# One encoder layer: the general program moved between the main program and the closing blocks, with branch hints

## The chip, the cores and the metric

The kernel runs on one core of one Trainium2 chip. The core has five engines with instruction streams of their own: TensorE (PE; its weight loads are listed as PEld), VectorE (DVE), ScalarE (ACT), GpSimd (POOL) and SyncE (SP), which here issues nearly all DMAs. Each stream is read by a sequencer, which also runs branches, register loads and semaphore waits itself; the profile marks such work with a q (SPq, PEldq). [...] The metric is the device time of one execution in microseconds (us), and a shorter time is better.

## The reference

The layer works on 1024 positions of width 1024 in float32. Two mixers run on one projection: dense grouped-query attention with axial rotary positions, and a mixture of three dilated windows with a distance penalty. A feed-forward network with a short convolution follows.

```python
def reference(x, norm1_g, w_in, ..., conv_w, conv_b, w_down):
    hn = rms_norm(x, norm1_g)
    proj = hn @ w_in
    ...
    out_a = global_gqa_attention(qa, ka, va)
    out_b = dilated_mixture_attention(rms_norm(qb, qb_norm_g), rms_norm(kb, kb_norm_g), vb)
    mixed = jnp.concatenate([rms_norm(out_a, outa_norm_g), rms_norm(out_b, outb_norm_g)], axis=-1)
    x = x + mixed @ w_out
    x = x + conv_ffn(rms_norm(x, norm2_g), w_up, conv_w, conv_b, w_down)
    return x
```

The queries and keys of both mixers are normalised per head and multiplied by gain vectors. So the gains alone bound how large a score before the softmax can become.

## The kernel before

The kernel holds the whole layer twice. The function `emit(bounded)` (L142) writes one complete program for all engines. With `bounded=True` it writes the main program, which leaves out the subtraction of the row maximum before the exponentials, since the scores are known to be small. With `bounded=False` it writes the general program, which subtracts it and then computes the whole output again.

Which one counts is decided on the chip. `bound()` (L597) computes from the gains, near the start, an upper bound of the scores and stores it in one element of the SBUF tile `bigf` at `O_LIM`. The main program always runs. After it, each of the five engines loads that element into a register (`values_load`, L1610) and compares it with a limit (`tc.If`, L1612). If the bound is above the limit, the engine goes on into the general program; with the inputs used here it is not, and the general program is skipped.

The built program of each engine consists of blocks that lie one behind the other in memory. Five blocks matter:
- a short opening block (L1668, L1672);
- the main program, which ends with the register load and the branch of the If. On SP it has 745 instructions;
- the closing block of the main arm (L1612). It waits until this engine's work, and on SP every DMA of the main program, is done, sets the semaphores to the values that the general program would have left, and jumps to the end. On SP it has 9 instructions: eight waits and the jump;
- the general program (L1612 stands for its branch too). On SP it has 729 instructions, on PE 7040 before weight loads are counted apart;
- the end (L1672). SP waits there for all semaphores with twelve waits and a drain, then all engines pass two barriers, between which POOL clears the semaphores. On SP it has 17 instructions.

Before the change they lie in this order: opening, main program, closing block, general program, end. The argument `preferred_fallthrough_block=False` asks for it: the arm taken when the condition is false follows the branch directly. So the branch of the If falls through into the closing block, and the closing block's jump to the end passes over the whole general program.

The work around the end of the main program is a product of the feed-forward network's second weight with the gated activations, by a scheme with seven products in place of eight block products (`steps`, `down`, L1474). Its last step adds four parts of the output and writes them: `out_add` (L1469) adds on DVE (L1470) and starts the write from SP (L1472). The order of instructions within a block comes from a scheduler that keeps each engine's dependencies; a call of no dependency is placed where the scheduler sees fit, not where it was written.

The profile calls both conditional branches and plain jumps COMPARE_BRANCH, waits on semaphores EVENT_SEMAPHORE, and the register load TENSOR_LOAD. The transfers that bring instructions to the engines are the queues of kind "instruction": q8 for PE and q14 for the other engines.

Of the kernel before, what the change touches and what calls it, by code (L numbers as in the profile page):

```python
# [41 lines left out]
O_LIM = O_F + 9232  # L42
LIMIT = 256.0
# [83 lines left out]
def tile_encoder_layer(ctx, tc, x, w_in, gains, outg, norm1_g, norm2_g, w_out, w_up, conv_w, conv_b,  # L127
                       w_down, ident, rope, tmx, tbc, cnt, tee, out):
    nc = tc.nc
# [3 lines left out]
    bigf = pool.tile([128, NF], F32, name="bigf")  # L133
# [8 lines left out]
    def emit(bounded):  # L142
# [930 lines left out]
        def take(prep, n):  # L1073
            for _ in range(n):
                if prep:
                    p = prep.pop(0)
                    if p:
                        p()
# [296 lines left out]
        def conv(j, u):  # L1375
            c = tile_of(j, u)
            i = F_U[2 * (j % 2) + u]
            a = acc(j, u)
            w = [f(O_CW + 44 * t + c, 1) for t in range(4)]
            act(f(a, 1024), f(i, 1024), AF.Identity, scale=w[1], bias=w[3])  # L1380
            for w_, o, d, n in ((w[0], 256, 0, 768), (w[0], 1, 768, 255), (w[2], 0, 256, 768), (w[2], 768, 1, 255)):
                vec.scalar_tensor_tensor(f(a + o, n), f(i + d, n), w_, f(a + o, n), op0=OP.mult, op1=OP.add)  # L1382

        def gate(j, u):
            a, v = acc(j - 1, u), acc(j, u)
            act(f(a, 1024), f(a, 1024), AF.Gelu_apprx_tanh)
            vec.tensor_tensor(f(v, 1024), f(a, 1024), f(v, 1024), op=OP.mult)
# [5 lines left out]
        def gate_sums(j):  # L1393
            e, o = acc(j, 0), acc(j, 1)
            s1, s3 = acc(j - 1, 0), acc(j - 1, 1)
            t = lambda d, a, b, op: gp.tensor_tensor(f(d, 512), f(a, 512), f(b, 512), op=op)
            g = gscr[j // 2]

            def behind_sum(o):

                gp.tensor_tensor(f(o, 1), f(F_S[1], 1), f(F_S[1], 1), op=OP.add)

            def halves():
                dma(g[:, 0:512], f(e, 512))
                dma(g[:, 512:1536], f(o, 1024))
                behind_sum(s1)
                t(s1, e + 512, o + 512, OP.add)

            def third():
                behind_sum(s3)  # L1410
                t(s3, e, e + 512, OP.subtract)

            def second():
                t(s1 + 512, s1, e, OP.subtract)
                dma(g[:, 1536:2560], f(s1, 1024))

            def fourth():
                t(s3 + 512, o, s1 + 512, OP.subtract)
                dma(g[:, 2560:3584], f(s3, 1024))

            return [halves, second, third, fourth]
# [5 lines left out]
        steps = [(n, q) for n in (1, 5, 6, 3, 7, 2, 4) for q in range(NQ)]  # L1427
# [4 lines left out]
        def d_load(m):  # L1432
            if m >= len(steps):
                return
            n, q = steps[m]
            o = F_DR[m % 4]
            dma(f(o, 512), w_part(q, *{1: (0, 0), 5: (0, 1), 6: (1, 1), 3: (1, 1), 7: (1, 1), 2: (1, 0), 4: (1, 0)}[n]))
            dma(f(o + 512, 512), gscr[q][:, place[n]:place[n] + 512])

        def d_load2(m):  # L1440
            n, q = steps[min(m, len(steps) - 1)]
            if n in (5, 7):
                dma(f(F_D2[q % 3], 512), w_part(q, 0, n == 7))

        def d_prep(m):
            if m >= len(steps):
                return
            n, q = steps[m]
            o, d, t = F_DR[m % 4], R_D[m % 6], F_T[q]
            sub = lambda out, i0, i1: vec.tensor_tensor(f(out, 512), f(i0, 512), f(i1, 512), op=OP.subtract)  # L1450
            if n == 5:
                sub(t, o, F_D2[q % 3])
            elif n == 6:
                sub(t, o, t)
            elif n == 7:
                sub(o, o, F_D2[q % 3])
            elif n == 4:
                sub(o, o, t)
            src = fp(t, [o + 512 - t, 2], [1, 512]) if n in (5, 6) else fp(o, [512, 2], [1, 512])
            act(rp(d, [512, 2], [1, 512]), src, AF.Copy)  # L1460
            vec.tensor_tensor(rp(d + 1024, [512, 2], [1, 512]), src, rfp(d, [512, 2], [1, 512]), op=OP.subtract)  # L1461
# [4 lines left out]
        def x_rows(c, t, tt, hf):  # L1466
            dma(f(c[t], 512), rscr[tt][:, 512 * hf:512 * hf + 512])

        def out_add(c, t, b, tt=None, hf=0):  # L1469
            vec.tensor_tensor(f(c[t], 512), bank(b), f(c[t], 512), op=OP.add)  # L1470
            if tt is not None:
                dma(o_rows(tt, hf), f(c[t], 512))  # L1472

        def down(m):  # L1474
            n, q = steps[m]
            d = R_D[m % 6]
            for t in range(4):
                o = bank(t + 4 * (n in (5, 3, 2)))
                ah, al = r(d + 512 + 128 * t, 128), r(d + 1536 + 128 * t, 128)
                mm(o, ah, r(d, 512), start=(q == 0 and n in (1, 5, 2)), stop=False, skip_group_check=True)  # L1480
                mm(o, ah, r(d + 1024, 512), start=False, stop=False, skip_group_check=True)  # L1481
                mm(o, al, r(d, 512), start=False, stop=(q == NQ - 1), skip_group_check=True)  # L1482
                if n == 4 and q == NQ - 1:
                    out_add(C_12, t, t, 4 + t, 0)

        def behind(n, q):

            if q < 4:
                if n == 5:
                    out_add(C_11, q, q)  # L1490
                elif n == 6:
                    out_add(C_22, q, 4 + q)
                elif n == 3:
                    out_add(C_12, q, q)
                elif n == 7:
                    out_add(C_12, q, 4 + q, q, 1)
                elif n == 2:
                    out_add(C_22, q, q, 4 + q, 1)
                elif n == 4:
                    out_add(C_11, q, 4 + q, q, 0)  # L1500
            elif 4 < q < 9:
                t = q - 5
                if n == 1:
                    x_rows(C_11, t, t, 0)
                elif n == 5:
                    x_rows(C_22, t, 4 + t, 1)
                elif n == 6:
                    x_rows(C_12, t, t, 1)
                elif n == 2:
                    x_rows(C_12, t, 4 + t, 0)  # L1510
# [83 lines left out]
        for m in range(len(steps)):  # L1594
            n, q = steps[m]
            down(m)
            d_prep(m + 3)
            if m < 2:
                conv(last, m)
            if m == 2:  # L1600
                gate(last, 0)
                gate(last, 1)
            if m == 3:
                take(gate_sums(last), 4)
            d_load2(m + 6)
            d_load(m + 7)
            behind(n, q)

    emit(True)
    limit = nc.values_load(bigf[0:1, O_LIM:O_LIM + 1].bitcast(mybir.dt.int32), min_val=0, max_val=2 ** 31 - 1,  # L1610
                           skip_runtime_bounds_check_because="any float32 that is not negative is right")
    with tc.If(limit > int(np.float32(LIMIT).view(np.int32)), preferred_fallthrough_block=False):  # L1612
        emit(False)


# [60 lines left out]
```

## Time and profile before

| what | value |
|---|---|
| median of three runs | 1301.46 us (1300.12 to 1302.01) |
| profiled execution, device time | 1300.51 us |
| its span, first to last instruction of the program | 1298.7 us |
| PE busy | 1236.4 us, 95% of the span |
| DVE, ACT, POOL busy | 70%, 49%, 30% |
| granted TensorE clock, mean | 0.988 |
| instruction transfers on q8 | 57, 0.93 MB |
| instruction transfers on q14 | 45, 0.37 MB |

The span covers the program's own instructions; the execution's time has 1.8 us more around it. An engine is counted as busy only for work in its datapath: branches, waits, register loads and the issue of DMAs are not busy time, so a stretch in which only sequencers run shows as idle. Rows by source line give, for each engine and operation, the count, the shortest, median and longest duration in ns, and the starts of the first and the last one in us from the start of the span.

### The profile page before, as it was taken

How to read it: one execution, taken by the hardware profiler on the slowest of the kernel's cores; microseconds unless marked ns; L12 is line 12 of the kernel's file. 1: busy time of each engine (PE TensorE's matmuls, PEld its weight loads, DVE VectorE, ACT ScalarE, POOL GpSimd, SP SyncE). 2: the span in 40 equal slices, each digit the busy share in tenths (PEclk: the TensorE clock that was granted, in tenths of full speed). 3: DMA queues.
4: the chain of work that ended last, by engine and by line, in shares of the span. 5: the costliest groups of instructions: out<-in, count | busy, mean ns of one | idle time of the engine just before them, and what ended most of it. 6: DMA issues, size and time to landing. Idle time of an engine off the chain costs nothing.

```text
span 1298.7 us, 18774 instructions
## 1 busy us (share of the span) xinstructions
PE 1236.4 (95%) x7063; PEld 1061.5 (82%) x7063; DVE 908.5 (70%) x1270; ACT 637.4 (49%) x1001; POOL 391.8 (30%) x300
## 2 busy tenths in 40 slices
PE   7999999999998889999999999999999998889996
PEld 7999998999997777888788888888888886657885
DVE  5988685124107779656999999999999964657672
ACT  7856554566556566535544453444443442234430
POOL 1610143000212230011465675665675530000000
PEclk9999999999999899999999999999999998999998
DMA  7126303000014444413222223232223357448970
GB/s 264 54 84 156 88 5 75 24 17 17 9 25 100 106 107 115 156 65 106 74 105 91 92 93 122 94 117 90 91 96 122 122 183 282 166 148 277 315 242 36
DMA packets 120935, 147.12 MB, mean 113 GB/s; under 512 B 51009, under 2 KB 79489, under 8 KB 120321
## 3 DMA queue, kind: packets, MB, share of 16 engines
q1 hardware_dynamic: 119617, 141.10, 33.6%
q0 software_dynamic: 1216, 4.72, 1.7%
q8 instruction: 57, 0.93, 0.3%
q14 instruction: 45, 0.37, 0.1%
HBM read 107.25 MB, written 33.82 MB: 109 GB/s over the span
## 4 chain that ended last, share of the span: by engine, by line
PE 55%; DVE 18%; issue 4%; DMA 4%; ACT 3%; POOL 1%; SPq 0%; ACTq 0%; DVEq 0%; POOLq 0%
PE ps L696 8%; PE ps L1349 6%; PE ps L1351 6%; PE ps L1350 6%; DVE bigf L1382 6%; PE ps L1481 4%; PE ps L1482 4%; PE ps L1480 4%; PE ps L701 3%; PE ps L702 2%; DVE bigf L1353 2%; PE ps L1004 2%; PE ps L1006 2%; PE ps L1005 2%; DVE bigr L1333 2%
## 5 line engine op out<-in xcount | busy, mean ns | idle before, releaser
L1349 PE MATMUL ps<-bigr 128*128 128x512 f32 x616 | 241.0, 391 | 6.5 <-DVE bigf L1353 5.9
L1350 PE MATMUL ps<-bigr 128*128 128x512 f32 x616 | 239.7, 389 | 0.0
L1351 PE MATMUL ps<-bigr 128*128 128x512 f32 x616 | 239.7, 389 | 0.0
L1382 DVE SCALAR_TENSOR_TENSOR bigf<-bigf 128x768 f32<-128x768 f32 (+1 forms) x176 | 178.8, 1074 | 26.5 <-ACT bigf L1380 26.4
L1332 ACT ACTIVATE bigr<-bigf 128x512 fp32r<-128x512 f32 x154 | 93.2, 625 | 139.3 <-POOL bigf L1324 70.4
L1460 ACT ACTIVATE bigr<-bigf 128x1024 fp32r<-128x1024 f32 x77 | 80.5, 1058 | 148.9 <-DMA bigf<-gscr 57.1
L1349 PEld LDWEIGHTS ps<-bigr 128*128 128x128 f32 x616 | 115.6, 188 | 35.1 <-DVE bigf L1353 9.3
L696 PEld LDWEIGHTS ps<-bigf 128*128 128x128 f32 x1024 | 131.9, 191 | 9.3 <-issue 0.3
L1351 PEld LDWEIGHTS ps<-bigr 128*128 128x128 f32 x616 | 115.6, 188 | 24.2
L1350 PEld LDWEIGHTS ps<-bigr 128*128 128x128 f32 x616 | 115.7, 188 | 23.5
L1461 DVE TENSOR_TENSOR bigr<-bigf,bigr 128x1024 fp32r<-128x1024 f32 x77 | 93.2, 1222 | 57.0 <-ACT bigr L1460 46.8
L1480 PE MATMUL ps<-bigr 128*128 128x512 f32 x308 | 114.1, 401 | 16.6 <-ACT bigr L1460 16.4
L696 PE MATMUL ps<-bigf 128*128 128x65 f32 x1024 | 129.1, 269 | 0.0
L421 PE MATMUL ps<-bigr 128*128 128x256 f32 x448 | 127.3, 284 | 1.2 <-ACT bigf L300 1.2
L1333 DVE TENSOR_TENSOR bigr<-bigf,bigr 128x512 fp32r<-128x512 f32 x112 | 125.3, 1136 | 3.2 <-ACT bigr L1332 2.5
L422 PE MATMUL ps<-bigr 128*128 128x256 f32 x448 | 126.9, 283 | 0.1
L423 PE MATMUL ps<-bigr 128*128 128x256 f32 x448 | 126.7, 283 | 0.0
L1481 PE MATMUL ps<-bigr 128*128 128x512 f32 x308 | 122.6, 400 | 1.4 <-DVE bigr L1461 0.9
L1482 PE MATMUL ps<-bigr 128*128 128x512 f32 x308 | 121.3, 395 | 0.0
L704 ACT ACTIVATE bigf<-ps 128x512 f32<-128x512 f32 x128 | 76.1, 597 | 78.9 <-PE ps L702 77.9
L421 PEld LDWEIGHTS ps<-bigr 128*128 128x128 f32 x448 | 85.8, 192 | 1.8 <-ACT bigf L300 1.6
L422 PEld LDWEIGHTS ps<-bigr 128*128 128x128 f32 x448 | 85.9, 192 | 0.3 <-DVE bigr L405 0.3
(215 smaller groups left out, 2441.8 us busy)
## 6 DMA issues: line engine op xcount, KB each, us to landing
bigf<-w_down SPq DMA_DIRECT2D x99, 256.0 KB, 3.7
bigf<-w_up SPq DMA_DIRECT2D x44, 512.0 KB, 3.6
bigf<-gscr SPq DMA_DIRECT2D x77, 256.0 KB, 3.7
gscr<-bigf SPq DMA_DIRECT2D x33, 512.0 KB, 2.6
bigf<-w_in SPq DMA_DIRECT2D x8, 1024.0 KB, 5.5
bigf<-x SPq DMA_DIRECT2D x15, 512.0 KB, 7.1
bigf<-w_out SPq DMA_DIRECT2D x8, 512.0 KB, 3.6
bigr<-bigr POOLq DMA_DIRECT2D x8, 512.0 KB, 4.7
```

The costliest lines, as they stand in the source:

```text
L421: mm(o, ah, wh, start=(k == 0 and t % 2 == 0 and n != 2), stop=False, skip_group_check=True)
L422: mm(o, ah, wl, start=False, stop=False, skip_group_check=True)
L423: mm(o, al, wh, start=False, stop=(k == 3), skip_group_check=True)
L696: mm(bank(ob, 65, 66 * i), f(slots[kt] + 128 * i, 128), f(F_VA + 132 * kt + 66 * kv, 65), start=(kt == 0 and i == 0), stop=(kt == 7), skip ...
L1333: (gp if n in (2, 4) and m > 3 else vec).tensor_tensor(rp(o + 512, [128, 4], [1, 128]), src, rfp(o, [128, 4], [1, 128]), op=OP.subtract)
L1349: mm(bank(b), wh, th, start=(k == 0 and n in (1, 5, 6, 7)), stop=False, skip_group_check=True)
L1350: mm(bank(b), wh, tl, start=False, stop=False, skip_group_check=True)
L1351: mm(bank(b), wl, th, start=False, stop=(k == 3), skip_group_check=True)
L1382: vec.scalar_tensor_tensor(f(a + o, n), f(i + d, n), w_, f(a + o, n), op0=OP.mult, op1=OP.add)
L1480: mm(o, ah, r(d, 512), start=(q == 0 and n in (1, 5, 2)), stop=False, skip_group_check=True)
L1481: mm(o, ah, r(d + 1024, 512), start=False, stop=False, skip_group_check=True)
L1482: mm(o, al, r(d, 512), start=False, stop=(q == NQ - 1), skip_group_check=True)
```

## The change

The If gets the opposite preference and a label, the register load is called inside the last loop of the main program, in the last step but one, and at the same place a branch hint is marked for all five engines. It names the label and says "likely taken".

```diff
             d_load2(m + 6)
             d_load(m + 7)
             behind(n, q)
-
+            if bounded and m == len(steps) - 2:
+                limit.append(nc.values_load(bigf[0:1, O_LIM:O_LIM + 1].bitcast(mybir.dt.int32), min_val=0,
+                                            max_val=2 ** 31 - 1, skip_runtime_bounds_check_because="any float32 that is not negative is right"))
+                tc.mark_branch_hint_location("general", "LikelyTaken", mybir.ALL_ENGINES)
+
+    limit = []
     emit(True)
-    limit = nc.values_load(bigf[0:1, O_LIM:O_LIM + 1].bitcast(mybir.dt.int32), min_val=0, max_val=2 ** 31 - 1,
-                           skip_runtime_bounds_check_because="any float32 that is not negative is right")
-    with tc.If(limit > int(np.float32(LIMIT).view(np.int32)), preferred_fallthrough_block=False):
+    limit, = limit
+    with tc.If(limit > int(np.float32(LIMIT).view(np.int32)), preferred_fallthrough_block=True, label="general"):
         emit(False)
```

In the built program the blocks then lie in the order opening, main program, general program, closing block, end. The branch of the If falls through into the general program and is taken to the closing block, which the end follows directly. Each engine's stream has one more instruction, the prefetch hint, which stands first in the main program's block and names that engine's branch of the If. All other instructions, their order within their blocks and the semaphores they wait for are the same, the register load among them: it stands behind the last matmul, addition and output write of its engine, as before.

## The prediction

> **What bounds the kernel now.** I read the page first, for the busy shares and the instruction queues, then the table by stage, then the end of the chain of waits, and then, line by line, what the sequencers do after the last arithmetic.
>
> ```profile
> span 1298.7 us, 18774 instructions
> ...
> PE 1236.4 (95%) x7063; PEld 1061.5 (82%) x7063; DVE 908.5 (70%) x1270; ACT 637.4 (49%) x1001; POOL 391.8 (30%) x300
> ...
> q8 instruction: 57, 0.93, 0.3%
> q14 instruction: 45, 0.37, 0.1%
> ```
>
> ```profile
> 1065.00:1287.70 222.70, 203.91 (x849) 160.11 (x847) 126.26 (x139) 70.24 (x67) 1.94 (x2) 0.97 0.65 218
> 1287.70:1298.70 11.00, 0.00 (x0) 0.00 (x0) 0.00 (x0) 0.00 (x0) 0.00 (x0) 0.70 0.17 60
> ```
>
> TensorE (PE) bounds the kernel as a whole, but the change does not touch what PE computes. In the table by stage the columns are busy time and count of PE, PEld, DVE, ACT and POOL. Its last row matters here: for the final 11.0 us no engine is busy at all. The chain of waits does not show these 11 us, because it follows engine work only. It ends with the four last additions of DVE:
>
> ```profile
> 1284.65 0.24 PE ps L1482
> 1284.89 0.02 issue
> 1284.92 2.73 DVE bigf L1470 x4
> ```
>
> So 1284.92 + 2.73 = 1287.65 is the end of arithmetic, and 1298.7 the end of the program. What lies between is SyncE (SP): the last write of the output, the branch of the If, the waits that close the main arm, and the waits that close the program. First the last output write:
>
> ```profile
> L1472 SPq DMA_DIRECT2D out_dram<-bigf x1: 333/333/333, 1287.7 to 1287.7; - x1
> ...
> DMA to landing us min/median/max: 4.5/4.5/4.5
> ```
>
> It lands at 1287.7 + 4.5 = 1292.2. The rows of the If (L1612, count, duration in ns, first and last start) and those of the program's end (L1672, in two adjoining windows, then the final barrier):
>
> ```profile
> L1612 SPq EVENT_SEMAPHORE  x8: 17/17/17, 1291.5 to 1292.6; - x8
> L1612 PEldq COMPARE_BRANCH  x2: 95/2182/4270, 1283.3 to 1287.1; - x2
> L1612 DVEq COMPARE_BRANCH  x2: 51/53/55, 1287.9 to 1288.1; - x2
> L1612 SPq COMPARE_BRANCH  x2: 38/46/53, 1288.6 to 1292.7; - x2
> ...
> L1612 DVEq EVENT_SEMAPHORE  x1: 21/21/21, 1288.0 to 1288.0; - x1
> ```
>
> ```profile
> L1672 SPq EVENT_SEMAPHORE  x3: 28/28/28, 1295.2 to 1295.4; - x3
> ```
>
> ```profile
> L1672 SPq EVENT_SEMAPHORE  x9: 27/28/28, 1297.2 to 1297.8; - x9
> L1672 SPq DRAIN  x1: 7/7/7, 1297.8 to 1297.8; - x1
> ```
>
> ```profile
> L1672 PEldq EVENT_SEMAPHORE  x2: 51/51/51, 1298.1 to 1298.7; - x2
> ```
>
> The SP sequence is: first branch at 1288.6 (the If, not taken); eight waits that let go as the output lands, 1291.5 to 1292.6; second branch at 1292.7 (past the general program to the end); nothing until 1295.2; three waits; nothing from 1295.4 to 1297.2; nine waits at 0.07 us each ((1297.8 − 1297.2) / 8); drain at 1297.8; barriers to 1298.7. The two silences are 2.5 and 1.8 us, in which SP waits for no semaphore that is still open: the last writes landed at 1292.2 and the other engines arrived earlier (below). They coincide with transfers on the instruction queue. The next table has DMA share and GB/s as its last two columns; 82 GB/s over 0.1 us is 8,192 bytes, which is what q14 moves at a time (0.37 MB / 45):
>
> ```profile
> 1292.80:1293.60 0.80, 0.50 0.00 0
> 1293.60:1293.70 0.10, 0.50 0.24 82
> 1293.70:1295.20 1.50, 0.50 0.00 0
> 1295.20:1295.70 0.50, 0.50 0.00 0
> 1295.70:1295.80 0.10, 0.50 0.25 82
> 1295.80:1297.30 1.50, 0.50 0.00 0
> ```
>
> So both silences are SP waiting for code. A jump to the end block fetches its 8 KB line (2.5 us), and since the block straddles two lines, its fourth wait stands in the next one. That one is asked for only about 0.5 us after the first is entered (1295.2 to 1295.7) and is usable 2.0 us after it (1295.2 to 1297.2).
>
> **The change, part by part.** The built program shows what moves. Instructions of the main program and both arms are the same on every engine and in the same order; SP has 745 in the main program, 9 in the closing block of the main arm, 729 in the general program and 17 at the end, before and after.
>
> *The register load.* It is called earlier, but keeps its place: on SP behind the last output write, on PE behind the last matmul, on DVE behind the last addition. Cost and gain nothing. Even a move would gain nothing, since on SP it lies under the landing at 1292.2.
>
> *The hints.* One prefetch hint per engine is added. They were marked in the last step but one, but in the built program each is its engine's first instruction. SP's first DMA issue and all that hangs on it shift by one such instruction. None is in the trace, so I bound it: below by 0.02 us (SP's waits, 17 ns), above by 0.10 us (PE's first branch, 95 ns). A gain from an extra instruction at the head of an idle queue is excluded. I take 0.05 us, near the SP rows, as SP starts the first transfers.
>
> *The order of the blocks.* Before: main program, closing block of the main arm, general program, end. After: main, general, closing block, end. On the path taken, the far jump goes from "closing block to end" to "If to closing block", and the end then follows the closing block directly. On SP this far jump now starts at 1288.6 and must be over when the third output write lands at 1291.5; before, it started at 1292.7 with nothing left to cover it.
>
> If the hint brings the target line in ahead, SP is in the closing block at once, and the next line, asked for 0.5 us after entry and usable 2.0 us after it, is there at about 1290.7, ahead of its use. Then:
> - first silence: 2.5 becomes one step of 0.07 to 0.1 us: −2.4
> - second silence: 1.8 becomes one step of 0.07: −1.7
> - hints: +0.05
>
> Sum: −4.05. Counted forward instead, from 1292.7 on: twelve waits of 0.07 (0.8), 0.9 us from drain to end and the hint's 0.05 put the end at 1294.5, which is −4.2. I take −4.1.
>
> The far jump of the other engines moves too, so I check that none becomes last. Their arrivals at the end block now:
>
> ```profile
> L1672 DVEq DRAIN  x1: 57/57/57, 1291.3 to 1291.3; - x1
> L1672 PEldq DRAIN  x1: 68/68/68, 1291.4 to 1291.4; - x1
> ```
>
> ```profile
> L1612 POOLq COMPARE_BRANCH  x2: 38/39/40, 1065.0 to 1067.8; - x2
> ...
> L1672 POOLq DRAIN  x1: 1128/1128/1128, 1071.7 to 1071.7; - x1
> ```
>
> ```profile
> L1672 ACTq DRAIN  x1: 80/80/80, 1274.6 to 1274.6; - x1
> ```
>
> PE pays its far jump in the record of the branch itself, 4270 ns from 1287.1; moved to its If at 1283.3 it would end at 1287.6, under matmuls already queued. DVE's takes 3.2 us (1288.1 to 1291.3) and would now start at 1287.9. POOL's 3.9 us (1067.8 to 1071.7) has over 200 us of cover. If DVE also needed its next line, 1287.9 + 3.2 + 2.0 = 1293.1, still before SP's drain at 1293.6. ACT is there by 1274.6. So SP stays last, and the whole gain counts.
>
> *Without the hint's help* the If's jump misses on SP. The price is 2.5 us by SP's own row at a quiet time, and 3.2 by DVE's, which ran like this one while the output was being written. I take 3.2 for this case, as the nearest in time: SP resumes at 1288.6 + 3.2 = 1291.8, 0.3 after the first landing but before the second. The next line is there at 1291.8 + 2.0 = 1293.8. The end block grows no longer, but all before it is one instruction longer by the hint, so the line ends after the second wait, at about 1292.9: a stall of 0.9. Then ten waits (0.7) and 0.9 to the end: 1295.4, or −3.3. With 2.5 it would be 1291.1, 1293.1, a stall of 0.2, and −4.0.
>
> [...]
>
> **The rivals.**
> 1. *The hint does nothing:* −3.3 plus the hint's 0.05, so 1301.46 − 3.2 = 1298.2. For it: nothing in the trace shows a hint at work, and it stands some 1290 us ahead of its branch. Against it: a hint names its branch, so distance alone need not matter.
> 2. *The second silence stays whole*, because the next line is not fetched while SP stands in waits: only the first 2.4 goes, less 0.05, so 1299.1. Against it: the fetch at 1295.7 came 0.5 us after entry while SP had done only three waits, so it looks tied to entry. A miss of 3.9 us like POOL's gives nearly the same: SP resumes at 1292.5, the next line is there at 1294.5, the end at 1296.1, so 1298.9.
> 3. *Slower:* the hint acts at once, at the top, and the line it fetches holds the place that the next sequential line needs, until the hinted branch runs. PE then meets its line ends uncovered, at up to 4.2 us each (4270 ns less a step). One such costs as much as the change gains, so 1301.5; two give 1305.7; all 57 of q8 some 240 us. It decides for slower by over 0.2% from 4.2 + 2.6 = 6.8 us on, that is from two late lines. For it: the first instruction is the earliest place there is. Against it: no place is shown to be short. [...]
> 4. *No change*, since the blocks lie otherwise when loaded than in the built program, or another wait ends at 1298.7: 1301.5. Against it: SP's silence at 1295.4 fits the block sizes as built.
>
> **How the numbers follow.** The profiled execution took 1300.51 us, 1.8 around its span of 1298.7, which the change does not touch; 0.95 below the median of the three runs, 1301.46, and inside their range, 1300.12 to 1302.01. Against the profiled execution the sum gives 1300.5 − 4.1 = 1296.4; against the median 1301.46 − 4.1 = 1297.4, which I predict. A measurement of this kernel can tell about 0.2%, 2.6 us, from no change, so the line is 1298.9.
>
> Chances: the forecast 0.60; rival 1 0.18; rival 2 0.08; rival 3 0.07; rival 4 and the rest 0.07. The forecast's own range is its sum, −4.0 to −4.2, with the runs' scatter of about 0.9 each way: 1296.4 to 1298.4. To reach 8 in 10 it takes in rivals 1 and 2: 1296.2 to 1299.5. Faster: nearly all of the forecast, three quarters of rival 1, a third of rival 2: 0.58 + 0.14 + 0.03 = 0.75. Slower: rival 3 but for a single late line: 0.06. The rest is the same: 0.19.
>
> **What would show it.** In the changed kernel's profile: five prefetch hints ahead of SP's first DMA issue, and that issue later by under 0.1 us; SP's eight waits of the If still from 1291.5 to 1292.6, then the twelve of the end without a gap to about 1293.6, and a span near 1294.5. If the hint works, PE's branch at 1283.3 is short and instruction transfers for the closing block come before 1287; if not, that branch takes some 4 us, and SP shows a gap of up to 1 us after the second wait of the end. Rival 2 shows a gap of 1.8 us there; rival 3 gaps on PE, each with a 16 KB instruction transfer that comes late. The prediction is wrong if anything but SP's code waits fills the last 6 us, or if the landing of the output moves because code is now fetched beside it.

## The result

The changed kernel takes 1295.69 us (median of six runs, 1293.65 to 1296.71), the kernel before, in runs beside it, 1301.3 us (1299.9 to 1304.06). The ratio is 0.9954, 95% interval 0.9941 to 0.9968. A second comparison later gave 0.9949 (0.9935 to 0.9963; medians 1295.44 and 1301.99). So it is faster by 0.5%, about 5.6 us, where 4.1 us were predicted; the predicted range of 1296.2 to 1299.5 ends 0.5 us above the measurement.

The profiled execution took 1296.54 us. Its page, its table by stage (busy time and count of PE, PEld, DVE, ACT, POOL, then clock, DMA share, GB/s) and the end of its chain of waits:

```profile
span 1294.7 us, 18774 instructions
...
q8 instruction: 56, 0.92, 0.3%
q14 instruction: 40, 0.33, 0.1%
```

```profile
1290.20:1294.70 4.50, 0.00 (x0) 0.00 (x0) 0.00 (x0) 0.00 (x0) 0.00 (x0) 0.63 0.36 134
```

```profile
1287.39 0.02 issue
1287.42 2.73 DVE bigf L1470 x4
```

The last addition ends at 1287.42 + 2.73 = 1290.15. What follows, which I call the tail, lasts 1294.75 − 1290.15 = 4.6 us; before it was 1298.70 − 1287.65 = 11.05 us. So the tail alone shrank by 6.45 us. In this pair of profiles the arithmetic ended 2.5 us later, which hides part of it. That is scatter: over all profiles below it ended between 1286.6 and 1292.3 us, the earliest in one with hints (everywhere but on DVE) and the latest in another (on SP alone), the four without a hint between 1287.6 and 1288.9. Since the tail is read inside one execution, it is free of that scatter, and the experiments go by it.

The rows of the last output write, of the If (now L1616) and of the end (L1676) show what became of SP's sequence:

```profile
L1472 SPq DMA_DIRECT2D out_dram<-bigf x1: 332/332/332, 1290.2 to 1290.2; - x1
...
DMA to landing us min/median/max: 2.4/2.4/2.4
```

```profile
L1616 SPq EVENT_SEMAPHORE  x8: 17/17/17, 1291.7 to 1293.1; - x8
L1616 PEldq COMPARE_BRANCH  x1: 423/423/423, 1285.8 to 1285.8; - x1
...
L1616 DVEq COMPARE_BRANCH  x1: 84/84/84, 1290.4 to 1290.4; - x1
L1616 DVEq EVENT_SEMAPHORE  x1: 21/21/21, 1291.0 to 1291.0; - x1
L1616 SPq COMPARE_BRANCH  x1: 70/70/70, 1291.2 to 1291.2; - x1
```

```profile
L1676 SPq EVENT_SEMAPHORE  x12: 28/28/28, 1293.1 to 1293.8; - x12
L1676 SPq DRAIN  x1: 7/7/7, 1293.9 to 1293.9; - x1
```

Both silences are gone: the eight waits of the closing block end at 1293.1, and the twelve of the end follow without a gap. The far jump now costs 0.5 us on SP (1291.2 to 1291.7) and 0.6 on DVE (1290.4 to 1291.0) instead of 2.5 and 3.2; on PE the branch takes 423 ns instead of 4270. And one thing stands there that was not forecast: the last output write lands 2.4 us after its issue, not 4.5.

The DMA share shows why. It is the mean over 16 DMA engines, so one engine busy alone is 0.06. Before (the arithmetic ended at 1287.65):

```profile
1287.70:1288.80 1.10, 1.00 0.98 367
1288.80:1289.40 0.60, 1.00 0.78 273
1289.40:1291.70 2.30, 1.00 0.06 18
```

After (it ended at 1290.15), the same stretches behind the end of the arithmetic:

```profile
1290.20:1291.30 1.10, 1.00 0.99 372
1291.30:1291.90 0.60, 0.57 0.80 294
1291.90:1294.20 2.30, 0.50 0.02 7
```

In both the write is nearly through 1.75 us after the arithmetic. Before, one single engine is then still busy for 2.3 us. Instruction transfers (count, MB, share of the DMA engines' time) in the 4.2 us behind the arithmetic, from 1287.6 before and then from 1290.1 after:

```profile
q8 instruction: 1, 0.02, 1.6%
q14 instruction: 1, 0.01, 0.5%
```

```profile
q14 instruction: 2, 0.02, 1.1%
```

Only before is there a line of PE (q8). The single packets in the trace show what it did. That line, 16,384 bytes, moves for 1,058 ns from 1288.9. From 1289.5, when the other engines are through, until the line ends at 1289.9, no packet of the output moves. Then sixteen of 2,048 bytes follow one behind another until 1291.7: one engine's share of the last two writes. The landing of the last write is told by sixteen signals in the trace: fifteen have come 2.4 us after its issue and the sixteenth at 4.5. So the line held up one of the sixteen engines, and the write counted as landed only with it. An 8,192-byte line (309 ns from 1289.5) moves at the same time; on which engine, the trace does not say.

Each hint stands at the top of its engine's stream, and SP's first issue comes 0.11 us later: about twice the 0.05 us that it was given, and just over the upper bound of 0.10. The hint in the changed kernel, then SP's first issue, before and after:

```profile
L1676 SPq BRANCH_PREFETCH_HINT  x1: 51/51/51, 0.7 to 0.7; - x1
```

```profile
0.73 0.40 SPq L568 DMA_DIRECT2D bigf<-ident  x1
```

```profile
0.84 0.39 SPq L568 DMA_DIRECT2D bigf<-ident  x1
```

### The profile page after: what moved, and what is told of

It is laid out like the page before. It is cut to its first block, busy times and chain, and to the rows that moved or that the text cites. A ratio compares the mean times of both kernels' runs of the same rounds, so it can differ in the third digit from the quotient of the medians.

```text
span 1294.7 us, 18774 instructions
## 1 busy us (share of the span) xinstructions
PE 1240.1 (96%) x7063; PEld 1065.0 (82%) x7063; DVE 907.9 (70%) x1270; ACT 637.2 (49%) x1001; POOL 391.7 (30%) x300
## 5 line engine op out<-in xcount | busy, mean ns | idle before, releaser
L1460 ACT ACTIVATE bigr<-bigf 128x1024 fp32r<-128x1024 f32 x77 | 80.4, 1058 | 148.7 <-DMA bigf<-gscr 56.4
```

## The experiments

Theory A says that what went is time in which code was fetched, in two places: SP's own waits for code, and PE's lines on a DMA engine that the output needed. Rival B says that the landing came out quicker for another reason or by chance, and the first rival of the prediction says that hints do nothing.

| kernel | tail, us | last write lands after | ratio to before (95% interval) |
|---|---|---|---|
| before | 11.05 | 4.5 | 1 |
| before, once more | 11.2 | 4.6 | one run |
| changed | 4.6 | 2.4 | 0.9954 (0.9941 to 0.9968) |
| changed, once more | 4.6 | 2.5 | 0.9949 (0.9935 to 0.9963) |
| new order, no hint | 7.9 | 3.6 | 0.9977 (0.9967 to 0.9988) |
| hint on SP alone | 6.3 | 4.1 | 0.996 (0.9943 to 0.9976) |
| hint not on SP | 6.2 | 2.5 | 0.9958 (0.9939 to 0.9976) |
| hint not on PE | 6.3 | 4.2 | 0.9968 (0.9954 to 0.9981) |
| hint not on DVE | 4.8 | 2.5 | 0.9953 (0.994 to 0.9966) |
| hint on PE and SP alone | 4.8 | 2.5 | 0.9945 (0.9926 to 0.9964) |
| old order, with hints | 11.05 | 4.5 | 1.0008 (0.9997 to 1.0018) |
| no If at all | 3.35 | 2.1 | 0.9946 (0.9927 to 0.9965) |

**The kernel before, once more.** No edit.

> The kernel before, once more, to see what in its last 11 us repeats. By the tail I mean the time from the end of the last addition on DVE (L1470) to the end of the span: 11.05 us before, 4.57 after. Theory A (instruction transfers share a DMA engine with the output write): the last output write lands 4.5 us after its issue again, and the tail is 11.0 +- 0.3. Rival B (the landing is slow or quick by chance): the landing is anywhere between 2.4 and 4.5 us, and the tail as short as 8.9.

The tail is 11.2 us, the landing 4.6 us, with the same two silences (2.5 and 2.0 us). The old order with hints, below, makes a third profile with a landing of 4.5, so chance is unlikely for the kernel before. The changed kernel was run once more too: a landing of 2.5 us and a tail of 4.6, where 2.4 +- 0.2 and 4.6 +- 0.2 were expected.

**The new order without hints.**

```diff
-                tc.mark_branch_hint_location("general", "LikelyTaken", mybir.ALL_ENGINES)
```

> The new order of the blocks without any hint. Theory A: the If's jump fetches on every engine; SP comes into the closing block 2.5 to 3.2 us after its branch, the fetches of PE and DVE fall into the output write, whose landing takes 3.5 to 4.5 us, and SP stalls once more at its line end. Tail 7 to 8 us, the time about 3 to 4 us under before. Rival (the hint does nothing, the order alone gives it all): tail 4.6 and the time equal to the changed kernel's, 5.5 us under before.

Tail 7.9 us. The rows of the If (here L1615) and, in two windows, of the end (L1675):

```profile
L1615 SPq EVENT_SEMAPHORE  x8: 17/17/17, 1292.2 to 1292.7; - x8
L1615 PEldq COMPARE_BRANCH  x1: 3678/3678/3678, 1284.0 to 1284.0; - x1
...
L1615 SPq COMPARE_BRANCH  x1: 50/50/50, 1289.3 to 1289.3; - x1
```

```profile
L1675 SPq EVENT_SEMAPHORE  x3: 28/28/28, 1292.8 to 1293.0; - x3
```

```profile
L1675 SPq EVENT_SEMAPHORE  x9: 28/28/28, 1294.7 to 1295.2; - x9
```

SP's jump takes 2.9 us (1289.3 to 1292.2), and after three waits of the end it stalls again for 1.7. The last write lands 3.6 us after its issue at 1288.3, so at 1291.9, before SP is there: here SP's own code decides the tail, not the landing. So the order alone gives half the gain, 3.2 us of tail, and the hint the other half. The prediction's first rival, a hint that does nothing, had put the changed kernel at just this, 3.2 us under before.

**The hint on SP alone.**

```diff
-                tc.mark_branch_hint_location("general", "LikelyTaken", mybir.ALL_ENGINES)
+                tc.mark_branch_hint_location("general", "LikelyTaken", [mybir.EngineType.SP])
```

> The changed kernel with the hint on SP alone. SP meets no fetch, so what is left is the landing. Theory A: the jumps of PE and DVE fetch while the output is being written, the landing takes 3 to 4.5 us, the tail 5.2 to 6.7. Rival B (landing independent of code transfers): landing 2.4 us and tail 4.6, as in the changed kernel.

The first line below is the landing of the last write, the second a count of instruction transfers from 1292.3 to 1294.3, the stretch of that write (the arithmetic ended at 1292.28):

```profile
DMA to landing us min/median/max: 4.1/4.1/4.1
```

```profile
q8 instruction: 1, 0.02, 5.2%
```

SP meets no fetch, and the tail is still 6.3 us, because the landing is back at 4.1: a 16 KB line of PE moves during the write.

**The hint on all engines but SP.**

```diff
+                tc.mark_branch_hint_location("general", "LikelyTaken", [e for e in mybir.ALL_ENGINES if e != mybir.EngineType.SP])
```

> The changed kernel with the hint on every engine but SP. Theory A: PE and DVE fetch nothing during the output write, the landing stays near 2.4 us; SP comes into the closing block 2.5 us after its branch and its next line 2.0 us later, so it stalls behind the second or third wait of the end: tail about 7. Rival (SP's hint does nothing, the other engines' hints give the whole gain): tail 4.6.

The landing stays at 2.5 us, and SP comes into the closing block late:

```profile
L1616 SPq EVENT_SEMAPHORE  x8: 17/17/17, 1294.4 to 1294.9; - x8
...
L1616 SPq COMPARE_BRANCH  x1: 45/45/45, 1291.4 to 1291.4; - x1
```

```profile
L1676 SPq EVENT_SEMAPHORE  x12: 28/28/28, 1295.0 to 1295.7; - x12
```

The jump takes 3.0 us. The stall that I expected behind the second or third wait does not come, so the tail is 6.2 and not 7. The edit leaves SP's own instructions as they are in the new order without hints, where it stalled.

**The hint on all engines but PE, and on all but DVE.** The edits are as the last, with PE or DVE in place of SP.

> The changed kernel with the hint on every engine but PE. Theory A, sharpened by the run with the hint on SP alone (landing 4.1 us, PE's following 16 KB line on its way during the write): PE's branch takes 3.7 us under queued matmuls, its next line is fetched from 0.4 us after the last addition on, the landing takes 4.1 +- 0.3 us and the tail 6.2 +- 0.3. Rival B (it was DVE's fetch, or chance): landing 2.4 us, tail 4.6.

> The changed kernel with the hint on every engine but DVE. Theory A: DVE's 8 KB line is asked for after its branch at 0.3 us and moves only when the output's share on that DMA engine is through, so the landing stays 2.4 to 2.8 us and the tail 4.6 to 5.0. Rival B: landing over 3 us, tail over 5.2.

First without PE's hint, then without DVE's:

```profile
L1472 SPq DMA_DIRECT2D out_dram<-bigf x1: 1727/1727/1727, 1289.4 to 1289.4; - x1
...
DMA to landing us min/median/max: 4.2/4.2/4.2
```

```profile
L1616 PEldq COMPARE_BRANCH  x1: 3362/3362/3362, 1285.0 to 1285.0; - x1
```

```profile
L1472 SPq DMA_DIRECT2D out_dram<-bigf x1: 332/332/332, 1286.6 to 1286.6; - x1
...
DMA to landing us min/median/max: 2.5/2.5/2.5
```

PE's hint decides the landing, 4.2 without it and 2.5 without DVE's. PE's missed branch itself stands under matmuls that are already queued (1285.0 to 1288.4, with the last write issued at 1289.4); what hurts is the line that PE fetches next, which moved from 0.3 us before the end of the arithmetic to 1.4 after it. SP was also longer in the issue of the last write, 1727 ns instead of 332, while that line moved; that the line held it is likely but not shown, since this happened in one profile only.

**Hints on PE and SP alone.**

```diff
+                tc.mark_branch_hint_location("general", "LikelyTaken", [mybir.EngineType.PE, mybir.EngineType.SP])
```

> The changed kernel with hints on PE and SP alone. Theory: these two carry the whole gain, PE's by keeping its lines out of the output write, SP's by letting it stand in the closing block when the output lands; the misses of DVE, ACT and POOL end before SP's drain. Tail 4.6 to 5.0, the time equal to the changed kernel's. Rival (every engine's fetch adds to the landing): tail over 5.2.

Tail 4.8 us, the time as with all five. Two hints carry the gain but for some 0.2 us of tail. DVE's jump over to its closing block and SP's waits of the end:

```profile
L1616 DVEq EVENT_SEMAPHORE  x1: 21/21/21, 1294.9 to 1294.9; - x1
```

```profile
L1676 SPq EVENT_SEMAPHORE  x12: 28/28/179, 1294.2 to 1295.0; - x12
```

One of SP's waits, the one for DVE, lasts 179 ns instead of 28: without its hint DVE comes into its closing block only at 1294.9, and is the last to arrive. In the kernel without DVE's hint the same wait lasts 133 ns. The landing, 2.5 us instead of 2.4, makes up the rest.

**The old order with hints.**

```diff
-    with tc.If(limit > int(np.float32(LIMIT).view(np.int32)), preferred_fallthrough_block=True, label="general"):
+    with tc.If(limit > int(np.float32(LIMIT).view(np.int32)), preferred_fallthrough_block=False, label="general"):
```

> The old order of the blocks with the hints of the changed kernel, which then call a branch likely that is not taken. Theory: the closing block lies in the same line as the branch on SP, so the wrong hint costs nothing there, and the jump to the end fetches as before: tail 11.1 +- 0.4, time as before. Rival: the wrongly fetched line has a price of one more fetch, tail 13 us or more, the time 2 us or more over before.

The tail is 11.05 us and the time that of before: a wrong hint cost nothing that can be measured (ratio 1.0008, 0.9997 to 1.0018), and brought nothing. The rows of the end in two windows:

```profile
L1676 SPq EVENT_SEMAPHORE  x2: 28/28/28, 1295.4 to 1295.5; - x2
```

```profile
L1676 SPq EVENT_SEMAPHORE  x10: 27/28/28, 1297.5 to 1298.0; - x10
```

SP stalls after the second wait of the end, where the kernel before stalled after the third. The one instruction that the hint adds has moved the line end by one, as the prediction's count had it.

**No If at all.** The load, the If and the second call of `emit` are taken out.

```diff
-    limit = nc.values_load(bigf[0:1, O_LIM:O_LIM + 1].bitcast(mybir.dt.int32), ...)
-    with tc.If(limit > int(np.float32(LIMIT).view(np.int32)), preferred_fallthrough_block=False):
-        emit(False)
```

> The main program alone: no register load, no If, no general program (left out: the second program for a bound above the limit, which these inputs do not need). It is the floor for everything that the If costs. No jump, no fetch out of line: landing 2.4 us, then only the waits of the end (0.8) and the barriers (0.9): tail 4.1 us, 0.5 under the changed kernel's. If the tail were well under that, more of the changed kernel's tail would belong to the If than its eight waits.

Tail 3.35 us, below the 4.1 expected: the landing is quicker still, 2.1 us, with no instruction transfer at all in the tail, and the end has nine SP waits instead of twelve. So everything that the If and the general program cost in the changed kernel's tail is 1.25 us, of 7.7 before. Nothing larger is left to take there.

## Why the prediction was right or wrong

**The place was right.** The last 11 us belonged to SP, not to arithmetic, and both silences, 2.5 and 1.8 us with one 8,192-byte instruction transfer in each, were waits for code. They went when the far jump was put under the landing of the output.

**The hint works, against the first rival.** The new order without it has a tail of 7.9 us, with it 4.6. The counts of transfers fit that. PE's queue q8 makes 57 transfers before and 56 after. In the packets, 55 of them come ahead of PE's branch in both kernels, the first some 25 us after the start; behind the branch come two in the kernel before and one in the changed kernel. So nothing more was fetched at the top, and yet the branch takes 423 ns, where it took 3678 without hints. What the 55 carry is not shown. My estimate from the counts is that one of them brought the branch's target in place of another line: most likely the last, 20 us ahead of the branch, since in the packets of the old order with hints just that one is missing. If so, PE's hint, which ran at 0.8 us, was acted on only some 1265 us later. Unhinted, the far jump took 2.4 us (ACT in the kernel before) to 4.4 us (PE in the old order with hints) in these runs.

**The failed step is the landing at 1292.2.** The prediction took 4.5 us from the last issue to the landing as given and counted SP's closing waits from there, so its sum holds the landing fixed: a term put at nothing. In fact 2.1 us of it were PE's line, fetched on account of the same far jump that the change moves. With 2.4 in its place the sum becomes −4.1 − 2.1 = −6.2, against a measured tail of −6.45 and a measured time of −5.6 (−6.55 in the second comparison), with the arithmetic's scatter in it. The runs with and without PE's hint show it: 2.4 to 2.5 us in the five profiles of the new order with it, 3.6 to 4.2 in the three without. The rows for it were at hand: the GB/s of the write's last 2.3 us were those of a single engine. The prediction did name a landing moved by code as a cause of failure, but only for code that is fetched newly, not for code that is no longer fetched.

**The second silence** went as forecast, but not as argued. The line should have ended behind the second wait of the end. And by the forecast's own count the next line, usable 2.0 us after SP came into the closing block at 1291.7, would have been there at 1293.7; SP reached the third wait at 1293.3, and a stall of some 0.4 us should have come. None came, so that the silence went in full is, as far as the argument goes, luck. In all six kernels with hints in the new order no line end was met within the twenty waits, even where SP has no hint; without hints, and with hints in the old order, it stood where the count put it. Whether the block lies differently in memory or its next line comes sooner is open; no run here shows it.

**The smaller terms.** The hint costs 0.11 us at the top, not 0.05. The register load gained nothing, as it did not move. POOL's and ACT's jumps stayed covered even without their hints, as the kernel with hints on PE and SP alone shows (tail 4.8 us). DVE's did in the changed kernel, but only because it was hinted: the prediction let it take until 1293.1 by setting it against an SP that waits for the slow landing, and with the quick one an unhinted DVE costs 0.10 to 0.15 us.

**The other rivals.** The second silence did not stay whole. No line of PE came late through a hint held for the whole program: the hinted kernels are faster by what their tails are shorter, as far as the scatter lets one tell. And the blocks do lie in the order as built: one branch per engine is left where there were two, and the end follows the closing block without a gap.

## What to carry to other kernels

Time behind the last arithmetic is in no chain of waits over engines; read it from the sequencers' rows, and look for instruction transfers in its gaps. Here the jump over the general program cost 2.4 to 4.3 us on every engine in the kernel before, with an instruction transfer in it. Where such a gap shows, put the jump under a wait that stands anyway, and hint it. And ask of every transfer that a change removes what else was queued on its DMA engine: here that was a third of the gain (2.1 of 6.45 us).

## What the runs showed of the hardware that was not expected

- In the kernel before, a code line of PE (one packet of 16,384 bytes, 1,058 ns) held up one DMA engine: fifteen of the last write's sixteen signals had come after 2.4 us, and the one behind the line after 4.5. In the tails shown here such a line took 0.9 to 1.7 us, and a 256 KB write beside it landed in 3.6 to 4.6 us instead of 2.1 to 2.5. In one profile SP was 1727 ns instead of 332 in the issue of a write while the line moved; the cause is not shown.
- With a branch hint on PE there are 55 transfers of its code ahead of the branch as before, and one behind it instead of two. A hinted far jump took 0.5 us on SP, 0.6 on DVE and 0.4 on PE; unhinted, 2.5 to 3.0 on SP, 3.2 to 3.5 on DVE and 3.4 to 4.4 on PE.
- A hint for a branch that is then not taken cost nothing measurable here (ratio 1.0008, 0.9997 to 1.0018).
